# Dilated attention of a hybrid encoder layer: strided scores by residue, softmax halves joined afterwards, projections interleaved

## The chip, the cores and the metric

The kernel runs on one core of a Trainium2 chip. The metric is the device time of one execution in microseconds; the kernel before has a median of 2906.49 us over three runs (2903.2 to 2910.44). All times in the sections up to the prediction come from these runs, from one profiled execution and from its trace.

Names of engines as the profile has them: PE is the matrix engine (PEld its weight loads), DVE the vector engine, ACT the scalar engine, POOL the GpSimd engine, SP the engine whose queue issues most DMAs.

## What is computed

One layer over 1024 tokens of width 2048, float32. The part that matters here is the attention group: 16 heads of width 64, with q and k partly rotated, and three dilated windows that are softmaxed separately and then mixed by their log-denominators (reference, cut):

```python
DILATION_CFG = ((128, 1), (512, 4), (2048, 16))
...
q = rope_partial(heads(aq, ATT_HEADS), pos) * (ATT_HD ** -0.5)
k = rope_partial(heads(ak, ATT_HEADS), pos)
v = heads(av, ATT_HEADS)
res = [dilated_band_attention(q, k, v, w, d) for (w, d) in DILATION_CFG]
outs = jnp.stack([r[0] for r in res])
lses = jnp.stack([r[1] for r in res])
alpha = jax.nn.softmax(lses, axis=0)
o_att = jnp.einsum('gbsh,gbshe->bshe', alpha, outs).reshape(B, S, ATT_W)
y_att = o_att * jax.nn.silu(ag.astype(f32))
```

In each window query i sees keys i + dilation*m with |m| <= 64, so 1, 4 and 16 are the steps. Mixing by the softmax of the log-denominators equals one softmax over all three windows with shared keys counted more than once. Both kernels use that: the windows of step 4 and 16 are one "strided" part (keys of the query's residue modulo 4, 256 of them, with log 2 added where both windows hold the key), and the window of step 1 is the "local" part (256 keys around a block of 128 queries). One softmax row has 512 entries, 256 of each part.

The rest of the layer: a norm, the input projection, an HGRN2 scan (8 heads), the output projection, norms and a gated embedding.

## The kernel before

The program is written with a planner: each engine's instructions are ordered at build time by their place in the program and by a modelled readiness, so that work that stands later in the program is moved ahead where an engine would be idle. Weight pieces are loaded with raised priority (`PRIO`).

Stages: the norm of x and its transposes (`prenorm`), v and the scan's values for all tokens (`v_group`), 8 scan heads (`hgrn`), 8 pairs of attention heads (`att`, 128 columns of q, k, v and gate each), then `w_out` and the gate products over token halves (`y_phase`, `g_phase`).

A projection of 128 columns is a "group" (`group_parts`, from L92): four weight pieces of 4x128 rows, each split into a high and a low fp32r part and a bf16 copy (`piece`, L75 load on SP, L82 ACT, L83 POOL, L84 DVE), each piece multiplied with both token halves in three forms (L101, L102, L106): 96 matmuls of 128x512. It is a generator: it yields twice per piece, so 8 times, after 12 matmuls on average. At its end a `sink` takes the two PSUM banks away. Four banks (`gb`) belong to groups, so two groups are open at most, and four (`wk`) to all else.

`att` does the following for a pair of heads. The k group ends in `sink_k`: `rope_evac` (L520 ACT, four small DMAs per half that swap rows, L527 POOL, L528 DVE), then a split of k into three bf16 parts (L580, L581, L586) and DMAs that copy each head's rows to the other half of the partitions (L582, L584), so that a contraction over 128 rows does two bf16 products at once. The q group does likewise (`sink_q`, `q_parts`), a quarter of the queries at a time. Then 16 units follow, one for each block i of 128 queries and head h (`score`): the strided part in 12 small matmuls (three split products of 32 queries for each of the four residues r; the four outputs stand at the partitions 32r), L634; the local part in three matmuls of 128 queries, L639; mask and row maximum (L645), exponent with row sum (L650), reciprocal (L652) and scaling (L653). Two units later `flip` transposes the 128x512 probabilities (L658, four transposes) and copies them out (L662, L664), and after each eight units `att_pv` multiplies them with the values (L542 strided, L556 local). The gate group (third projection of the pair) is begun before the units (five yields), and its rest stands at the end of the pair's code; the planner takes its matmuls in between the units.

Of the kernel before, what the change touches and what calls it, by code (L numbers as in the profile page):

```python
# [2 lines left out]

# [41 lines left out]
class Kern:  # L45
# [367 lines left out]
    def att_consts(self, positions):  # L413
# [17 lines left out]
        bf = sp.tile([128, 1], F32, name="abf", bufs=1)  # L431
        V.tensor_copy(bf, b)
        tf = sp.tile([128, 1], F32, name="atf", bufs=1)
        V.tensor_copy(tf, tl)
        MK = big.tile([128, 864], F32, name="amask")
        e = self.h2("ae").bitcast(I32)[:, :480]
        nc.gpsimd.iota(e, pattern=[[1, 480]], base=-224, channel_multiplier=0)
        d = self.h2("ad")[:, :480]
        V.tensor_scalar(d, e, bf, None, op0=ALU.subtract)
        V.tensor_copy(e, d)  # L440
        V.tensor_scalar(e, e, 3, None, op0=ALU.bitwise_and)
        c2 = self.h2("ac2")[:, :480]
# [3 lines left out]
        m = MK[:, :480]  # L446
        V.tensor_tensor(m, d, c2, op=ALU.mult)
        V.tensor_tensor(d, d, c2, op=ALU.max)
        V.tensor_scalar(d, d, -NEG, NEG, op0=ALU.mult, op1=ALU.add)
        V.scalar_tensor_tensor(m, m, math.log(2.0), d, op0=ALU.mult, op1=ALU.add)  # L450
        e2 = self.h2("ae2").bitcast(I32)[:, :384]
        nc.gpsimd.iota(e2, pattern=[[1, 384]], base=-128, channel_multiplier=0)
        m = MK[:, 480:]
# [3 lines left out]
        V.tensor_scalar(m, m, -NEG, NEG, op0=ALU.mult, op1=ALU.add)  # L457
# [57 lines left out]
    def rope_evac(self, is_q, hf, src, fin):  # L515
        nc = self.nc
        sl = slice(512 * hf, 512 * hf + 512)
        raw = self.h2("araw")
        sc = 0.125 if is_q else 1.0
        nc.scalar.activation(raw, src, AF.Copy, scale=sc)  # L520
        pt = self.part[self.npart % 2]
        self.npart += 1
        for o in (0, 64):
            nc.sync.dma_start(pt[o:o + 8, :], raw[o + 8:o + 16, :])
            nc.sync.dma_start(pt[o + 8:o + 16, :], raw[o:o + 8, :])
        pr = self.h2("apr")
        nc.gpsimd.tensor_tensor(pr, pt, self.RS[:, sl], op=ALU.mult)  # L527
        nc.vector.tensor_tensor(raw, raw, self.RC[:, sl], op=ALU.mult)  # L528
        fin(raw, pr)
# [5 lines left out]
    def att_pv(self, hf, PT, vc, vn, vix, wstart, yt):  # L535
        nc = self.nc
        o = self.wk("ao")
        ov = o.rearrange("p (i r b) -> p i r b", i=4, r=4)
        for r in range(4):
            for k in range(2):  # L540
                for h in range(2):
                    nc.tensor.matmul(ov[64 * h:64 * h + 64, :, r, :], vc[:, r, k, 64 * h:64 * h + 64],  # L542
                                     PT[h][:, :, k, 32 * r:32 * r + 32], start=(r == 0 and k == 0), stop=False, skip_group_check=True)
        groups = {}
        for i in range(4):
            for ch in range(2):
                groups.setdefault((wstart(4 * hf + i) + 128 * ch), []).append((i, 2 + ch))
        gl = list(groups.items())
        for n, (t, lst) in enumerate(gl):
            for h in range(2):  # L550
                i, ca = lst[0]
                if len(lst) == 2:
                    mv = sap(PT[h][:, :, :, :], i * 512 + 384, [[384, 2], [1, 128]])
                else:
                    mv = PT[h][:, i, ca]
                nc.tensor.matmul(o[64 * h:64 * h + 64, 128 * i:128 * i + 128 * len(lst)], vn[:, vix[t], 64 * h:64 * h + 64], mv,  # L556
                                 start=False, stop=(n == len(gl) - 1), skip_group_check=True)
        nc.scalar.copy(yt[:, 512 * hf:512 * hf + 512].rearrange("p (i b r) -> p i r b", i=4, r=4), ov)


    def att(self, w_in, hp, vsrc, yout):
        nc = self.nc
        V = nc.vector
        big = self.big
        ident = self.ident
        base = 128 * hp
        KS = [big.tile([128, 2, S], BF16, name=f"ak{i}", tag=t, bufs=n) for i, (t, n) in enumerate((("X", 2), ("X", 2), ("O", 1)))]
        QT = big.tile([128, 2, 2, 2, 256], BF16, name="aqt", tag="hv", bufs=1)
        nat = (slice(0, 64), slice(64, 128))

        def sink_k(hf, p):
            def fin(a, b):
                sl = slice(512 * hf, 512 * hf + 512)
                V.tensor_tensor(a, a, b, op=ALU.add)
                for s in range(3):
                    for h in range(2):
                        n, m = nat[h], nat[1 - h]
                        kd = KS[s][n, h, sl]
                        if s < 2:
                            nc.scalar.copy(kd, a[n])  # L580
                            V.tensor_tensor(a[n], a[n], kd, op=ALU.subtract)  # L581
                            nc.sync.dma_start(KS[s][m, h, sl], kd)  # L582
                            if s == 0:
                                nc.sync.dma_start(KS[2][m, h, sl], kd)  # L584
                        else:
                            V.tensor_copy(kd, a[n])  # L586
            self.rope_evac(False, hf, p, fin)

        qn = {}

        def sink_q(hf, p):
            def fin(a, b):
                qn[hf] = self.h2("aq")
                V.tensor_tensor(qn[hf].rearrange("p (i r b) -> p i b r", i=4, r=4),
                                a.rearrange("p (i b r) -> p i b r", i=4, r=4),
                                b.rearrange("p (i b r) -> p i b r", i=4, r=4), op=ALU.add)
            self.rope_evac(True, hf, p, fin)

        def q_parts(j):
            q = qn[j // 2][:, 256 * (j % 2):256 * (j % 2) + 256]  # L600
            for h in range(2):
                n = nat[h]
                qd = QT[n, j % 2, h]
                nc.scalar.copy(qd, q[n, None, :].to_broadcast([64, 2, 256]))
                V.tensor_tensor(q[n], q[n], qd[:, 0], op=ALU.subtract)
            t = big.tile([128, 2, 256], BF16, name="aq23", tag="hacc", bufs=1)
            nc.scalar.copy(t[:, 0], q)
            V.tensor_tensor(t[:, 1], q, t[:, 0], op=ALU.subtract)
            for h in range(2):
                nc.sync.dma_start(QT[nat[1 - h], j % 2, h], t[nat[h]])  # L610

        starts = [0, 128] + [128 * j - 64 for j in range(1, 8)] + [768, 896]
        vix = {t: i for i, t in enumerate(starts)}
        vn = big.tile([128, 11, 128], F32, name="avn", tag="ht", bufs=1)
        vc = big.tile([128, 4, 2, 128], F32, name="avc", tag="hvt", bufs=1)
        for i0, n in ((0, 2), (2, 7), (9, 2)):
            t0 = starts[i0]
            nc.sync.dma_start(vn[:, i0:i0 + n], vsrc[t0:t0 + 128 * n, :].rearrange("(c p) e -> p c e", p=128))
        for k in range(2):
            nc.sync.dma_start(vc[:, :, k], vsrc[512 * k:512 * k + 512, :].rearrange("(p r) e -> p r e", r=4))  # L620
        self.group(w_in, 1024 + base, sink_k)
        self.flush()
        self.group(w_in, base, sink_q)
        q_parts(0)
        q_parts(1)

        yt = big.tile([128, S], F32, name="ayt", tag="gt", bufs=1)
        def score(i, h, sm, first):
            w0 = wstart(i)
            sc = self.wk("asc")  # L630
            qb = QT[:, (i // 2) % 2, h, :, 128 * (i % 2):128 * (i % 2) + 128]
            for s, sq in ((0, 0), (1, 0), (2, 1)):
                for r in range(4):
                    t = nc.tensor.matmul(sc[32 * r:32 * r + 32, :256], qb[:, sq, 32 * r:32 * r + 32],  # L634
                                     KS[s][:, h, r::4], start=(s == 0), stop=False, skip_group_check=True)
                    if first is not None and s == 0:
                        self.after(t, first)
            for s, sq in ((0, 0), (1, 0), (2, 1)):
                nc.tensor.matmul(sc[:, 256:], qb[:, sq], KS[s][:, h, w0:w0 + 256], start=False, stop=(s == 2), skip_group_check=True)  # L639
            ms = 32 * (7 - i)  # L640
            mw = 480 + (w0 - 128 * i + 128)
            mx = self.sp.tile([128, 1], F32, name="amx")
            mk = sap(self.MK[:, :], ms, [[mw - ms, 2], [1, 256]])
            smh = sm[:, h]
            V.tensor_tensor_reduce(out=smh.rearrange("p (a b) -> p a b", a=2), in0=sc.rearrange("p (a b) -> p a b", a=2),  # L645
                                    in1=mk, scale=1.0, scalar=-3.0e38, op0=ALU.add, op1=ALU.max, accum_out=mx)
            nm = self.sp.tile([128, 1], F32, name="anm")
# [30 lines left out]
        for _ in range(5):  # L678
            mm = next(gpart)
# [348 lines left out]
```

## Time and profile before

| | us |
|---|---|
| median of three runs | 2906.49 |
| the profiled execution's own time | 2911.69 |
| its span, first to last instruction | 2909.9 |
| PE busy in it | 2785.7 (96%) |
| DVE, ACT, POOL busy | 1508.4, 925.5, 1023.8 |
| attention before the first `w_out` matmul, 1268.32 to 2050.83 | 782.51, of which PE busy 770.88 |
| one pair of heads, from the same point of one to that of the next | 101.1 |

A busy share is the time that an engine had an instruction in flight. Matmuls overlap in flight (one of 128x512 shows some 390 ns and the next begins some 227 ns later), so what a matmul costs the PE is read from the starts of neighbours, not from its duration.

### The profile page before, as it was taken

Reading aid. Unit: us, or ns where it says so; the run is one execution under the profiler, and the core shown is the slowest. Engines: PE = TensorE matmul, PEld = TensorE weight load, DVE = VectorE, ACT = ScalarE, POOL = GpSimd, SP = SyncE. Lnnn points to the kernel's source line nnn. Section 1 sums busy time; section 2 is a strip of 40 time slices with the busy share of each in tenths; the row PEclk is TensorE's granted clock in tenths of the full one; section 3 lists DMA queues with packets and bytes.
Section 4 is the critical chain, followed back from the end, with each engine's and each line's share of the span. In section 5 each row is a group of like instructions: output and inputs, shape, how many; then the busy total and the mean of one; then the engine's idle time right before and its main releaser. Section 6 shows DMA issues by size and latency. Waiting matters only on the chain. (4 is left out here: it accounts for less than half of the span.)

```text
span 2909.9 us, 46582 instructions
## 1 busy us (share of the span) xinstructions
PE 2785.7 (96%) x18128; PEld 1885.7 (65%) x18384; DVE 1508.4 (52%) x2833; ACT 925.5 (32%) x1672; POOL 1023.8 (35%) x769
## 2 busy tenths in 40 slices
PE   6999999999999999999999999999999899999997
PEld 4666666676667676676666666666566566665664
DVE  8601116856346346356655555555755645555555
ACT  5311112222122112124434444443533223333323
POOL 2422223413313313322222222222244554666555
PEclk9999999999999999999999999999999999999998
DMA  6412221211111111121221222122344543433453
GB/s 226 121 55 80 77 86 39 66 52 39 57 52 44 52 52 45 51 65 55 78 70 45 73 76 71 47 74 71 113 122 133 159 142 97 131 113 109 146 155 106
DMA packets 251614, 250.54 MB, mean 86 GB/s; under 512 B 21633, under 2 KB 175233, under 8 KB 250241
## 3 DMA queue, kind: packets, MB, share of 16 engines
q1 hardware_dynamic: 242224, 238.62, 27.6%
q10 hardware_dynamic: 9168, 8.93, 0.9%
q8 instruction: 144, 2.36, 0.3%
q14 instruction: 78, 0.63, 0.1%
HBM read 205.54 MB, written 29.36 MB: 81 GB/s over the span
## 5 line engine op out<-in xcount | busy, mean ns | idle before, releaser
L83 POOL TENSOR_TENSOR wl<-raw,wh 128x512 fp32r<-128x512 f32 x568 | 764.7, 1350 | 1599.8 <-ACT wh L82 1507.1
L84 DVE CAST wb<-raw 128x512 bf16<-128x512 f32 x584 | 430.5, 740 | 785.2 <-PE gb L106 281.8
L82 ACT CAST wh<-raw 128x512 fp32r<-128x512 f32 x584 | 358.4, 617 | 1241.7 <-PE gb L101 414.7
L101 PE MATMUL gb<-uh,wh 128*128 128x512 f32 x1792 | 744.3, 415 | 0.0
L102 PE MATMUL gb<-uh,wl 128*128 128x512 f32 x1792 | 708.6, 395 | 0.0
L106 PE MATMUL gb<-ul,wb 128*128 128x512 bf16 x1632 | 405.7, 380 | 9.8 <-issue 1.8
L101 PEld LDWEIGHTS gb<-uh,wh 128*128 128x128 f32 x1792 | 337.1, 188 | 82.9 <-issue 1.2
L102 PEld LDWEIGHTS gb<-uh,wl 128*128 128x128 f32 x1792 | 337.1, 188 | 68.9 <-issue 1.0
L106 PEld LDWEIGHTS <-wb 128*128 128x128 bf16 x1792 | 158.4, 98 | 204.6 <-issue 54.3
L810 PE MATMUL gb<-wh,yh 128*128 128x512 f32 x512 | 231.2, 452 | 2.8 <-DVE Y L842 2.8
L810 PE MATMUL gb<-wh,th 128*128 128x512 f32 x480 | 215.8, 450 | 0.0
L811 PE MATMUL gb<-wl,yh 128*128 128x512 f32 x512 | 203.7, 398 | 4.7 <-POOL wl L83 4.7
L811 PE MATMUL gb<-wl,th 128*128 128x512 f32 x480 | 190.6, 397 | 5.4 <-POOL wl L83 5.4
L645 DVE CUSTOM_DVE_ANT_1 asm<-asc,amask 128x512 f32<-128x512 f32 x128 | 88.3, 690 | 119.9 <-PE asc L639 119.7
L814 PE MATMUL gb<-wb,yl 128*128 128x512 bf16 x479 | 133.7, 383 | 1.6
L814 PE MATMUL gb<-wb,tl 128*128 128x512 bf16 x452 | 126.2, 384 | 1.0
L650 ACT ACTIVATE asm<-asm,anm 128x512 f32<-128x512 f32 x128 | 92.5, 722 | 90.3 <-DVE anm L648 90.0
L810 PEld LDWEIGHTS gb<-wh,yh 128*128 128x128 f32 x512 | 97.6, 191 | 33.3 <-DVE Y L842 3.3
L737 PE MATMUL gb<-wh,uh 128*128 128x512 f32 x256 | 116.4, 461 | 1.4 <-ACT wh L82 1.3
L811 PEld LDWEIGHTS gb<-wl,yh 128*128 128x128 f32 x512 | 97.4, 190 | 24.3 <-POOL wl L83 5.9
L738 PE MATMUL gb<-wl,uh 128*128 128x512 f32 x256 | 102.4, 407 | 10.9 <-POOL wl L83 7.9
L634 PE MATMUL asc<-ak,aqt 128*32 128x256 bf16 x1536 | 109.7, 401 | 3.2 <-issue 2.4
(274 smaller groups left out, 3668.4 us busy)
## 6 DMA issues: line engine op xcount, KB each, us to landing
raw<-in_w_in_dram SPq DMA_DIRECT2D x320, 256.0 KB
raw<-in_w_out_dram SPq DMA_DIRECT2D x128, 256.0 KB
raw<-in_w_pg_dram SPq DMA_DIRECT2D x128, 256.0 KB
xt<-in_x_dram SPq DMA_DIRECT2D x8, 1024.0 KB
vD<-vo SPq DMA_DIRECT2D x32, 256.0 KB
raw<-yD SPq DMA_DIRECT2D x32, 256.0 KB
xr<-in_x_dram SPq DMA_DIRECT2D x32, 256.0 KB
ak<-ak SPq DMA_DIRECT2D x96, 64.0 KB
```

Source lines behind the costliest of these rows:

```text
L82: nc.scalar.copy(wh, raw)
L83: (sub or nc.gpsimd).tensor_tensor(wl, raw, f32(wh), op=ALU.subtract)
L84: nc.vector.tensor_copy(wb, raw)
L101: nc.tensor.matmul(pb[hf], wh[:, k], self.uh[hf][:, kt], start=(kt == 0), stop=False)
L102: nc.tensor.matmul(pb[hf], wl[:, k], self.uh[hf][:, kt], start=False, stop=False)
L106: mm = nc.tensor.matmul(pb[hf], wb[:, k], self.ul[hf][:, kt], start=False, stop=(kt == KT - 1))
L634: t = nc.tensor.matmul(sc[32 * r:32 * r + 32, :256], qb[:, sq, 32 * r:32 * r + 32], KS[s][:, h, r::4], start=(s == 0), stop=False, skip_gr ...
L737: nc.tensor.matmul(pb[t], hi, wh, start=(k == 0), stop=False)
L738: nc.tensor.matmul(pb[t], hi, wl, start=False, stop=False)
L810: nc.tensor.matmul(pb[t], a, pc[0], start=first, stop=False)
L811: nc.tensor.matmul(pb[t], a, pc[1], start=False, stop=False)
L814: nc.tensor.matmul(pb[t], lo[:, k, 128 * t:128 * t + 128], pc[2], start=False, stop=last)
```

## The change

Only the attention group is changed.

The strided scores are computed for 128 queries of one residue at a time: a half of the tokens (512) holds 128 queries of each residue, so one full product of 128 queries and 256 keys takes the place of four products of 32 queries. The queries are therefore laid out by residue (`(r i b)` in place of `(i r b)`), and the local products take a copy (`ql`) of them in the old order, made by ACT or POOL. A unit is now (part, i) and holds both heads: six matmuls into one bank.

The rows of the strided and of the local part of a query now stand in different units and on different partitions. Each unit takes its own row maximum and sum over 256 entries; afterwards maxima and sums are copied across between the two layouts (16 small copies), and factors are worked out that join the two (minimum, differences, one exponent, sums, reciprocal). The signs of the scores and masks are turned round, so that the extreme is a minimum and serves as the exponent's bias directly. The scaling by the factors stands in `values`, half of it on ACT and half on DVE, ahead of the transposes.

`att` is replaced by a class `Pair` and an order written out at the bottom: the scores of a half take four yields of a group between their units; the next pair's q group and k group stand inside the pair's own code, the k group ahead of the second `values`; the gate group is spread over the pair.

```diff
-        MK = big.tile([128, 864], F32, name="amask")
+        MK = big.tile([128, 768], F32, name="amask")
...
-        sc = 0.125 if is_q else 1.0
+        sc = -0.125 if is_q else 1.0
...
+        def q_half(self, hf):
...
+            for c in range(2):
+                cs = slice(256 * c, 256 * c + 256)
+                for h in range(2):
+                    n = nat[h]
+                    qd = QT[n, h, :, cs]
+                    nc.scalar.copy(qd, q[n, None, cs].to_broadcast([64, 2, 256]))
+                    V.tensor_tensor(q[n, cs], q[n, cs], QT[n, h, 0, cs], op=ALU.subtract)
...
+        def scores(self, hf, fill):
+            K, KS, QT = self.K, self.KS, self.QT
...
+            for u, (loc, i) in enumerate(((0, 0), (0, 1), (1, 0), (0, 2), (1, 1), (0, 3), (1, 2), (1, 3))):
+                w0 = K.wstart(4 * hf + i)
+                sc = K.wk("asc")
+                if loc:
+                    ql = K.big.tile([128, 4, 4, 32], BF16, name="aql", tag="aql", bufs=3)
+                    src = QT.rearrange("p h s (r i b) -> p (h s) r i b", i=4, r=4)[:, :, :, i]
+                    (nc.gpsimd.tensor_copy if i % 2 else nc.scalar.copy)(ql, src)
+                for h in range(2):
+                    for s, sq in ((0, 0), (1, 0), (2, 1)):
+                        if loc:
+                            st = ql[:, 2 * h + sq].rearrange("p r b -> p (r b)")
+                            mv = KS[s][:, h, w0:w0 + 256]
+                        else:
+                            st = QT[:, h, sq, 128 * i:128 * i + 128]
+                            mv = KS[s][:, h, i::4]
+                        nc.tensor.matmul(sc[:, 256 * h:256 * h + 256], st, mv, start=(h == 0 and s == 0),
+                                         stop=(s == 2), skip_group_check=True)
...
+                for h in range(2):
+                    d = sm[h][:, loc, i]
+                    V.tensor_tensor_reduce(out=d, in0=sc[:, 256 * h:256 * h + 256], in1=K.MK[:, ms:ms + 256], scale=1.0,
+                                           scalar=3.0e38, op0=ALU.add, op1=ALU.min, accum_out=own[:, 0, loc, h, i:i + 1])
+                    nc.scalar.activation(d, d, AF.Exp, scale=-1.0, bias=own[:, 0, loc, h, i:i + 1],
+                                         accum_out=own[:, 1, loc, h, i:i + 1])
+                if u % 2:
+                    next(fill, None)
+            for x in range(4):
+                for y in range(4):
+                    o = oth[32 * x:32 * x + 32].rearrange("p s l h i -> p (s l h) i")[:, :, y]
+                    w = own[32 * y:32 * y + 32].rearrange("p s l h i -> p (s l h) i")[:, :, x]
+                    V.tensor_copy(o, w)
...
+            nc.scalar.activation(e, e, AF.Exp)
...
+        def values(self, hf):
...
+            def turn(n):
+                l, i = steps[n]
+                p = K.wk("apt", (128, 2, 2, 128))
+                for h in range(2):
+                    d = sm[h][:, l, i]
+                    if h:
+                        nc.scalar.activation(d, d, AF.Copy, scale=f[:, l, h, i:i + 1])
+                    else:
+                        V.tensor_scalar(d, d, f[:, l, h, i:i + 1], None, op0=ALU.mult)
+                    for c in range(2):
+                        nc.tensor.transpose(p[:, h, c], d[:, 128 * c:128 * c + 128], K.ident)
+                if n % 2 == 0:
+                    pt[n // 2] = K.big.tile([128, 2, 2, 2, 128], F32, name="aPT", tag=("KD", "hq")[n // 2 % 2], bufs=1)
+                (nc.scalar.copy if n % 2 else V.tensor_copy)(pt[n // 2][:, n % 2], p)
...
+            for n in range(10):
+                if n < 8:
+                    turn(n)
+                if n >= 2:
+                    use(n - 2)
...
-        for hp in range(8):
-            K.att(w_in, hp, vD[hp // 4][:, 128 * (hp % 4):128 * (hp % 4) + 128], yD[hp])
+        heads = [K.Pair(K, w_in, hp, vD[hp // 4][:, 128 * (hp % 4):128 * (hp % 4) + 128], yD[hp]) for hp in range(8)]
+
+        def run(parts, n=8):
+            for _ in range(n):
+                next(parts, None)
+
+        run(heads[0].queries(), 9)
+        K.flush()
+        run(heads[0].keys(), 9)
+        heads[0].q_half(0)
+        for n, a in enumerate(heads):
+            b = heads[n + 1] if n < 7 else None
+            a.loads()
+            g = a.gate()
+            if n == 0:
+                run(g, 4)
+            a.scores(0, g)
+            bq = b.queries() if b else iter(())
+            run(bq, 4)
+            if n == 7:
+                run(g, 2)
+            a.q_half(1)
+            a.values(0)
+            a.scores(1, bq if b else islice(g, 2))
+            run(bq)
+            if b:
+                if n:
+                    run(g, 2)
+                run(b.keys(), 9)
+                b.q_half(0)
+            a.values(1)
+            run(g)
```

`use(n)` multiplies step n's transposed probabilities with the values, four matmuls of 64 columns each (two key blocks, two heads), strided steps with `vc` and local ones with `vn`, all into one bank. `keys`, `queries`, `gate` and `loads` issue what `sink_k`, `sink_q`, `sink_g` and the value loads issued before.

More of the change, by code (lines that the diff above doesn't have):

```diff
@@ L2 @@
 from contextlib import ExitStack, nullcontext
+from itertools import islice
 import numpy as np
@@ L430, in att_consts @@
         V.tensor_tensor(tl, tl, rho, op=ALU.add)
-        bf = sp.tile([128, 1], F32, name="abf", bufs=1)
-        V.tensor_copy(bf, b)
+        pf = sp.tile([128, 1], F32, name="apf", bufs=1)
+        V.tensor_copy(pf, p_i)
         tf = sp.tile([128, 1], F32, name="atf", bufs=1)
         V.tensor_copy(tf, tl)
-        MK = big.tile([128, 864], F32, name="amask")
[L436 to L439, printed above, removed]
+        MK = big.tile([128, 768], F32, name="amask")
+        e = self.h2("ae").bitcast(I32)[:, :384]
+        nc.gpsimd.iota(e, pattern=[[1, 384]], base=-128, channel_multiplier=0)
+        d = self.h2("ad")[:, :384]
+        V.tensor_scalar(d, e, pf, None, op0=ALU.subtract)
         V.tensor_copy(e, d)
         V.tensor_scalar(e, e, 3, None, op0=ALU.bitwise_and)
-        c2 = self.h2("ac2")[:, :480]
+        c2 = self.h2("ac2")[:, :384]
         V.tensor_scalar(c2, e, 0, None, op0=ALU.is_equal)
@@ L445, in att_consts @@
         V.tensor_scalar(d, d, 64.0 * 64.0, None, op0=ALU.is_le)
-        m = MK[:, :480]
+        m = MK[:, :384]
         V.tensor_tensor(m, d, c2, op=ALU.mult)
         V.tensor_tensor(d, d, c2, op=ALU.max)
-        V.tensor_scalar(d, d, -NEG, NEG, op0=ALU.mult, op1=ALU.add)
-        V.scalar_tensor_tensor(m, m, math.log(2.0), d, op0=ALU.mult, op1=ALU.add)
+        V.tensor_scalar(d, d, NEG, -NEG, op0=ALU.mult, op1=ALU.add)
+        V.scalar_tensor_tensor(m, m, -math.log(2.0), d, op0=ALU.mult, op1=ALU.add)
         e2 = self.h2("ae2").bitcast(I32)[:, :384]
         nc.gpsimd.iota(e2, pattern=[[1, 384]], base=-128, channel_multiplier=0)
-        m = MK[:, 480:]
+        m = MK[:, 384:]
         V.tensor_scalar(m, e2, tf, None, op0=ALU.subtract)
@@ L456, in att_consts @@
         V.tensor_scalar(m, m, 64.0 * 64.0, None, op0=ALU.is_le)
-        V.tensor_scalar(m, m, -NEG, NEG, op0=ALU.mult, op1=ALU.add)
+        V.tensor_scalar(m, m, NEG, -NEG, op0=ALU.mult, op1=ALU.add)
         self.MK = MK
@@ L533, in after @@
                                reason="issue order")
[L535 to L539, printed above, removed]
-            for k in range(2):
-                for h in range(2):
[L542 to L558, printed above, removed]
@@ L561, in att @@
[L561 to L572, printed above, removed]
-                sl = slice(512 * hf, 512 * hf + 512)
[L574 to L647, printed above, removed]
-            V.tensor_scalar(nm, mx, -1.0, None, op0=ALU.mult)
-            den = self.sp.tile([128, 1], F32, name="aden")
-            nc.scalar.activation(smh, smh, AF.Exp, bias=nm, accum_out=den)
-            rd = self.sp.tile([128, 1], F32, name="ard")
-            V.reciprocal(rd, den)
-            return V.tensor_scalar(smh, smh, rd, None, op0=ALU.mult)
-        def flip(i, h, sm, PT, mark):
-            p = self.wk("apt", (128, 4, 128))
-            for c in range(4):
-                t = nc.tensor.transpose(p[:, c], sm[:, h, 128 * c:128 * c + 128], ident)
-                if c == 0 and mark is not None:
-                    self.after(t, mark)
-            if h == 0:
-                nc.scalar.copy(PT[h][:, i % 4], p)
-            else:
-                V.tensor_copy(PT[h][:, i % 4], p)
-        def wstart(i):
-            return 0 if i == 0 else (768 if i == 7 else 128 * i - 64)
-        def sink_g(hf, p):
-            sl = slice(512 * hf, 512 * hf + 512)
-            sg = self.h2("sg")
-            nc.scalar.activation(sg, p, AF.Sigmoid)
-            V.tensor_tensor(sg, p, sg, op=ALU.mult)
-            nc.gpsimd.tensor_tensor(sg, sg, yt[:, sl], op=ALU.mult)
-            nc.sync.dma_start(yout[:, sl], sg)
-        gpart = self.group_parts(w_in, 3072 + base, sink_g)
-        for _ in range(5):
-            mm = next(gpart)
-        PTs = {}
-        sms = {}
-        marks = []
-        dist = 2
-        units = [(i, h) for i in range(8) for h in range(2)]
-        for u in range(16 + dist):
-            if u < 16:
-                i, h = units[u]
-                if h == 0:
-                    if i in (2, 4):
-                        q_parts(i // 2 + 1)
-                    sms[i] = big.tile([128, 2, 512], F32, name="asm", tag=("KD", "hq")[i % 2], bufs=1)
-                marks.append(score(i, h, sms[i], mm if u == 0 else None))
-            if u >= dist:
-                pi, ph = units[u - dist]
-                if pi % 4 == 0 and ph == 0:
-                    PTs[pi // 4] = [big.tile([128, 4, 4, 128], F32, name=f"aPT{g}", tag=("F2", "Q2")[g], bufs=1) for g in range(2)]
-                flip(pi, ph, sms[pi], PTs[pi // 4], marks[min(u, 15)])
-                if pi % 4 == 3 and ph == 1:
-                    self.att_pv(pi // 4, PTs[pi // 4], vc, vn, vix, wstart, yt)
-        for _ in gpart:
-            pass
```

117 lines of the change are left out of this document (added).

## The prediction

> **What bounds the kernel now.** I read the page's engine table first, then the stretches of the attention stage, then the PE's waits in it.
>
> ```profile
> span 2909.9 us, 46582 instructions
> PE 2785.7 (96%) x18128; PEld 1885.7 (65%) x18384; DVE 1508.4 (52%) x2833; ACT 925.5 (32%) x1672; POOL 1023.8 (35%) x769
> ```
>
> ```profile
> 1500.34:1601.46 101.12, 99.78 (x698) 65.79 (x705) 56.14 (x135) 45.58 (x85) 24.58 (x19) 1.00 0.23 65
> ...
> 1904.62:2005.70 101.08, 99.74 (x698) 65.78 (x705) 55.81 (x135) 45.70 (x85) 24.58 (x19) 1.00 0.23 65
> ```
>
> ```profile
> PE apt L658 <- DVE asm L653: 3.7, 6, 0.6
> ```
>
> The two rows of stretches are one pair of heads each (columns: length, then busy time of PE, PEld, DVE, ACT, POOL, the granted clock, DMA share, GB/s). Of 101.1 us the PE is busy for 99.75, at full clock; DVE has 56, ACT 46, POOL 25, and the DMAs 0.23. The largest wait that the PE's own list names in the whole stage sums to 3.7 us. So here the time is the PE's instruction stream, and an edit is worth what it takes out of that stream, less what it makes the PE wait.
>
> **The stream of a pair, priced by starts.** Durations overlap, so I price by the starts in the timeline.
>
> ```profile
> 1279.20 0.58 PE L101 MATMUL gb<-uh,wh 128*128 128x512 f32 x1
> ...
> 1284.60 0.58 PE L101 MATMUL gb<-uh,wh 128*128 128x512 f32 x1
> ```
>
> ```profile
> 1342.86 0.60 PE L658 MATMUL apt<-ident,asm 128*128 128x128 f32 x4
> 1343.39 0.87 PE L634 MATMUL asc<-ak,aqt 128*32 128x256 bf16 x12
> 1344.19 0.50 PE L639 MATMUL asc<-ak,aqt 128*128 128x256 bf16 x3
> 1344.45 0.48 PE L101 MATMUL gb<-uh,wh 128*128 128x512 f32 x1
> 1344.76 0.39 PE L102 MATMUL gb<-uh,wl 128*128 128x512 f32 x1
> 1344.99 0.40 PE L101 MATMUL gb<-uh,wh 128*128 128x512 f32 x1
> ```
>
> ```profile
> 1369.67 1.85 PE L542 MATMUL ao<-aPT,avc 128*64 128x128 f32 x29
> ...
> 1373.30 0.39 PE L639 MATMUL asc<-ak,aqt 128*128 128x256 bf16 x2
> ```
>
> ```profile
> L634 PE MATMUL asc<-ak,aqt 128*32 128x256 bf16 x192 | 13.7, 400 | 0.1
> L658 PE MATMUL apt<-ident,asm 128*128 128x128 f32 x67 | 9.9, 273 | 0.6 <-DVE asm L653 0.6
> L639 PE MATMUL asc<-ak,aqt 128*128 128x256 bf16 x48 | 8.2, 276 | 0.0
> L542 PE MATMUL ao<-aPT,avc 128*64 128x128 f32 x64 | 4.8, 277 | 0.0
> L556 PE MATMUL ao<-aPT,avn 128*64 128x128 f32 x32 | 3.2, 273 | 0.0
> L556 PE MATMUL ao<-aPT,avn 128*64 128x256 f32 x16 | 2.5, 379 | 0.0
> ```
>
> - Groups: one weight piece (24 matmuls) takes 1284.60 - 1279.20 = 5.40 us, so one yield 2.70 us, one group 21.6, three groups 64.8.
> - Strided scores: 1344.19 - 1343.39 = 0.80 us for 12 instructions; 16 units make 12.8.
> - Local scores: 0.26 us for three, and the way back to the group costs 0.31 - 0.23 = 0.08 more: 0.34, so 0.114 for one full product; 16 units make 5.4.
> - Transposes: 1343.39 - 1342.86 = 0.53 for four. Their starts lie (0.60 - 0.27)/3 = 0.11 apart, so 0.09 of it is the change to another shape. 16 sets make 8.5.
> - Values: 3.6 us for all but two instructions of a half, some 3.8 with them: 7.6.
>
> The sum is 99.1, plus 1.3 not busy, against 101.1; the rest is other changes of shape.
>
> **The change, part by part.**
>
> *Strided products.* Of 192 instructions of 32 queries and 48 local ones 96 full products are left. At 0.114 each they cost 10.9 where 18.2 stood: -7.3 us a pair, -58 over eight. What the trace doesn't show is a full product whose keys are read with a step of four. The bounds come from these two rows:
>
> ```profile
> L634 PE MATMUL asc<-ak,aqt x1536: 384/405/418, 1330.4 to 2109.2; 128*32 128x256 bf16 x192
> L639 PE MATMUL asc<-ak,aqt x384: 272/273/421, 1331.2 to 2109.7; 128*128 128x256 bf16 x192
> ```
>
> A small product with stepped keys is in flight 405 - 273 = 132 ns longer than a full one with contiguous keys of the same length. If that is the price of four outputs fed at once from four places, it goes. If it is the price of the step, it stays on 384 products: +51 us, which leaves 7. In between I take the first, for the reason in these rows of the scan (four small products at once too, float32):
>
> ```profile
> L275 PE MATMUL pl<-Q,X x64: 210/213/221, 470.5 to 471.2; 128*32 128x32 f32 x64
> L275 PE MATMUL pl<-Q,X x64: 192/196/217, 473.8 to 474.4; 128*32 128x32 f32 x64
> ```
>
> The first reads a moving operand that jumps by some 4 KB at each element, the second one that jumps after every two, and only the first is longer. A far jump for each two elements costs nothing there, and the keys' step is 8 bytes. It is an argument, not a measurement.
>
> The Trainium skill has a rule on either side. "SBUF — State Buffer" (Specifications) says that memory lines of 16 bytes give full bandwidth from two hits on; the scan's two rows agree, and by it the step is free and the sum stays at -58. "TensorE: Matmul & The Clock Gate" (Measured speedup vs the span model) says that tiles side by side take the time of one and about 4 ns for each further one; by it the four outputs were free already, the 132 ns are the step's, and the sum would be -7. The trace's 0.80 us for three sets of four disagree with that span, but not on whose fault it is.
>
> *Values.* Transposes and value products keep their volume: 64 transposes; 128 instructions of 128 columns, where 64 + 32 + 16 double ones stood. But now each of 16 steps changes from transposes to products and back, one change of 0.09 more per step: +1.5 a pair, +12. Against it the 0.114 counts a way back to the group for each three products, 32 a pair, where the written order has 8 (after each second unit): 24 x 0.08 = -1.9 a pair, -15. I let these two cancel.
>
> *Softmax beside the PE.* Rows of one pair:
>
> ```profile
> L650 ACT ACTIVATE asm<-asm,anm 128x512 f32<-128x512 f32 x16 | 11.6, 723 | 12.2 <-DVE anm L648 12.1
> L650 ACT ACTIVATION_READ_ACCUMULATOR asm<-asm,anm 128x1 f32 x16 | 3.0, 186 | 0.0
> L82 ACT CAST wh<-raw 128x512 fp32r<-128x512 f32 x12 | 7.4, 614 | 13.5 <-PE gb L101 11.9 <-POOL apr L527 1.6
> L607 ACT CAST aq<-aq 128x256 bf16<-128x256 f32 x4 | 1.6, 401 | 4.6 <-DMA aqt<-aq 4.1 <-DVE aq L605 0.6
> L645 DVE CUSTOM_DVE_ANT_1 asm<-asc,amask 128x512 f32<-128x512 f32 x16 | 11.1, 692 | 16.8 <-PE asc L639 16.8
> L648 DVE TENSOR_SCALAR anm<-amx 128x1 f32<-128x1 f32 x16 | 2.4, 148 | 0.3
> ```
>
> An exponent of 256 columns lies between 0.36 (half) and 0.72; from 0.614 and 0.401 for 512 and 256 I take 0.723 - 0.213 = 0.51. ACT then has 32 x (0.51 + 0.19) = 22.3 for 14.6, plus 16 scalings at 0.40 and four query copies at 0.61: 45.6 + 7.7 + 6.4 + 2.4 = 62 of some 94 us. DVE has 32 maxima at 0.49 (the same proportion) for 16 at 0.69, loses 16 of the 0.148 operations, 16 reciprocals and half the scaling, and gains some 50 tiny operations at 0.15: it stays under 60. POOL's two copies a half are hidden behind the first yield between the units. None is a bound, and in one half's scores ACT's 16 x 0.70 + 1.2 = 12.4 us stand beside 5.5 of products and 10.8 of four yields.
>
> *Joining.* Sixteen copies across, for which the trace has no row (between 0 and 0.148 each, the nearest row, which I take), nine small operations and an exponent: some 4.2 us after the last unit. Ahead of the first `values` stand four yields (10.8), ahead of the second two yields and the k group (27): hidden, and 4.2 x 16 = 67 us if no cover stood there.
>
> *Groups moved.* The k group issues four weight loads, eight row-swapping DMAs and twelve key copies on SP; it goes from ahead of the pair's own units to the end of the pair before. `loads` waits for the last value products on the same queue, and the next pair's weight pieces stand behind it. What is late next is the key's way from its group to the first score:
>
> ```profile
> L520 ACT ACTIVATE araw<-gb x2: 575/576/577, 1383.1 to 1387.1; 128x512 f32<-128x512 f32 x2
> L582 SPq DMA_DIRECT2D ak<-ak x8: 461/540/548, 1394.4 to 1413.1; - x8
> ```
>
> ```profile
> L520 ACT ACTIVATE araw<-gb x2: 589/593/597, 1415.2 to 1420.1; 128x512 f32<-128x512 f32 x2
> ...
> 1431.46 0.85 PE L634 MATMUL asc<-ak,aqt 128*32 128x256 bf16 x12
> ```
>
> Keys took 30 us (1383.1 to 1413.1), with nobody waiting; the first half of the queries, for which the PE did wait, 16.3 (1415.2 to 1431.46). Both halves of the keys are needed at once, and the halves begin 4.9 apart: I estimate 21. The cover is `values` of the second half, 8 x 0.53 + 3.8 = 8.0, and two gate yields, 5.4: 13.4; with the next pair's first four gate yields, which depend on nothing in it, 24.2. The planner has moved such matmuls forward before: the k group that is evacuated from 1383.1 on is the second pair's, and the first pair's value products of its first half stand at 1369.67, so half of that pair's units were still to come. So I charge 1 us a pair: +8.
>
> **Sum.** -58 + 12 - 15 is taken as -58; + 8 gives -50. The profiled execution took 2911.69 (span 2909.9): 2861.7. The median of the runs lies 5.2 below that execution: 2856.
>
> **Rivals.**
>
> 1. *Step at a loss:* the 132 ns belong to the step. For it: the small products' longer flight is the only trace of stepped bf16 keys. Against: the scan's rows. With 132 ns it gives 2856 + 51 = 2907; with the shortest flight of the row, 384 - 273 = 111 ns, 2899; and without the waits that I charged 2891: I take 2899, between no change and barely faster. The Trainium skill's "TensorE: Matmul & The Clock Gate" stands on this rival's side, "SBUF — State Buffer" against it.
> 2. *Keys late, the slower side:* the key's way, 25 us (between 21 and 30), finds only the 13.4 of its own pair's cover, because weight pieces queue behind `loads`: 11.6 at seven pair boundaries, +81, less the 8 charged: 2929. It decides from (58/7 =) 8.3 us of lateness a pair. For it: SP issues in order. Against: only 1.3 us of a pair is idle now under the same planner.
> 3. *More than forecast:* no new wait, the cancelled terms fall to the good side, and the 1.3 idle goes: 2856 - 8 - 3 - 10 = 2835.
>
> **Chances.** Forecast 0.60, first rival 0.18, second 0.14, third 0.08. What can be told from no change is 0.3%, 8.7 us: under 2897.8 is faster, over 2915.2 slower. Faster: 0.60 + 0.08, and half of the first rival with its bounds, 0.08: 0.76. Same: the rest of that rival and the mild end of the second, 0.11. Slower: 0.13. The range 2828 to 2906 leaves out the second rival and the ends of the others.
>
> **What would show it.** Right: stretches of a pair of 94 to 95 us with the PE still over 98% busy; strided products of 273 ns in flight, starts 0.11 apart. Rival 1: the strided form near 400 ns, the local one at 273. Rival 2: PE idle before the first strided product of each pair, released by a key copy's DMA or by DVE. The joining would be wrong if the first transposes of `values` wait for DVE's or ACT's scaling by several us.

## The result and the profile after

The changed kernel takes 2933.41 us (median of four runs, 2930.28 to 2936.55), the kernel before 2908.47 beside it: a ratio of 1.0088 with a 95% interval of 1.0068 to 1.0108. It is slower by some 25 us. The forecast was 2856 and faster. Medians here and below are over runs at a granted clock of 0.98 to 0.99; one execution of the experiment with a fixed table, at 0.558 and 4581.4 us, is left out.

The page of the changed kernel (engine table), and two pairs of heads from its view of stretches (length, then busy time of PE, PEld, DVE, ACT and POOL, clock, DMA share, GB/s):

```profile
span 2929.7 us, 45661 instructions
PE 2793.9 (95%) x17360; PEld 1906.6 (65%) x17360; DVE 1541.4 (53%) x3265; ACT 1022.2 (35%) x2094; POOL 1045.4 (36%) x801
```

```profile
1733.76:1836.92 103.16, 98.77 (x578) 68.17 (x577) 62.72 (x190) 57.33 (x138) 27.89 (x23) 1.00 0.25 67
...
1940.00:2043.14 103.14, 99.42 (x578) 68.60 (x577) 62.38 (x189) 56.98 (x137) 27.67 (x23) 0.98 0.24 64
```

A pair takes 103.1 us where it took 101.1, with some 120 PE instructions fewer. The PE is no longer busy all the time in it: in the two shown 4.4 and 3.7 us are idle where it was 1.3. DVE and ACT are at 62 and 57, about as reckoned; neither is full.

The two forms of score product in the changed kernel (the three numbers with strokes are the least, the median and the greatest flight in ns):

```profile
L642 PE MATMUL asc<-ak,aqt x384: 385/407/437, 1337.1 to 2088.8; 128*128 128x256 bf16 x192
L642 PE MATMUL asc<-ak,aql x384: 270/273/421, 1337.5 to 2090.3; 128*128 128x256 bf16 x192
```

Same line of the program, same shape, the queries on the left of equal size: the strided form (`aqt`) flies 407 ns, the local one (`aql`) 273. In the timeline they stand like this:

```profile
1743.76 1.53 PE L642 MATMUL asc<-ak,aqt 128*128 128x256 bf16 x6
...
1748.52 1.47 PE L642 MATMUL asc<-ak,aql 128*128 128x256 bf16 x12
```

Six strided products are (1.53 - 0.41)/5 = some 0.225 us apart, twelve local ones (1.47 - 0.27)/11 = 0.109.

What the PE waited for from the end of the scan to the last values, with total, times and longest in us:

```profile
PE asc L642 <- DMA ak<-ak: 16.4, 6, 3.9
PE ao L707 <- ACT aPT L697: 6.8, 5, 1.6
PE asc L642 <- ACT sg L727: 4.5, 2, 2.4
PE apt L694 <- DVE asm L692: 4.2, 3, 2.1
```

Before, the same stretch named 4.2 for the scaling (L653) and 3.1 for a copy of transposes, and 2.4 at the very first score.

To put both effects into one account I took each PE instruction's time from its start to the next one's start, from the last scan output to the first gate product, and counted what goes over 0.48 us as waiting (less 0.24 for the instruction itself):

| us | before | after | difference |
|---|---|---|---|
| whole stretch | 1201.5 | 1223.3 | +21.8 |
| score products | 145.4 | 125.0 | -20.4 |
| transposes | 66.0 | 70.1 | +4.1 |
| value products | 65.6 | 70.9 | +5.3 |
| waiting | 26.4 | 58.6 | +32.2 |
| groups and the rest | 898.1 | 898.7 | +0.6 |

So the scores gave a third of what was reckoned, and waits took more than that back. The experiments go after each.

### The profile page after: what moved, and what is told of

The parts are those of the page before. It is cut to its first block, busy times and chain, and to the rows that moved or that the text cites. A ratio compares the mean times of both kernels' runs of the same rounds, so it can differ in the third digit from the quotient of the medians.

```text
span 2929.7 us, 45661 instructions
## 1 busy us (share of the span) xinstructions
PE 2793.9 (95%) x17360; PEld 1906.6 (65%) x17360; DVE 1541.4 (53%) x3265; ACT 1022.2 (35%) x2094; POOL 1045.4 (36%) x801
## 5 line engine op out<-in xcount | busy, mean ns | idle before, releaser
L85 DVE CAST wb<-raw 128x512 bf16<-128x512 f32 x584 | 406.3, 699 | 769.6 <-PE gb L107 276.5
L107 PE MATMUL gb<-ul,wb 128*128 128x512 bf16 x1792 | 434.8, 381 | 0.2 <-issue 0.2
L647 DVE CUSTOM_DVE_ANT_0 asm<-asc,amask 128x256 f32<-128x256 f32 x256 | 95.8, 422 | 125.0 <-PE asc L642 124.1
L649 ACT ACTIVATE asm<-asm,aown 128x256 f32<-128x256 f32 x256 | 127.3, 498 | 58.1 <-DVE aown L647 57.9
L642 PE MATMUL asc<-ak,aqt 128*128 128x256 bf16 x384 | 96.8, 405 | 20.9 <-DMA ak<-ak 16.4
```

The source lines that it names most:

```text
L85: nc.vector.tensor_copy(wb, raw)
L107: mm = nc.tensor.matmul(pb[hf], wb[:, k], self.ul[hf][:, kt], start=False, stop=(kt == KT - 1))
L649: nc.scalar.activation(d, d, AF.Exp, scale=-1.0, bias=own[:, 0, loc, h, i:i + 1], accum_out=own[:, 1, loc, h, i:i + 1])
```

## Experiments

### The step of the keys

First the same kernel with neighbouring keys in the strided products:

```diff
-                            mv = KS[s][:, h, i::4]
+                            mv = KS[s][:, h, 256 * i:256 * i + 256]
```

> The changed kernel, but each strided product reads 256 neighbouring keys (256*i on) in place of every fourth one; the scores are then of other keys than the reference's, the amount of work is the same. Theory A (the step of the keys doubles a product's time): in flight 273 ns in place of 405, starts 0.11 us apart in place of 0.21, so 384 x 0.10 = 38 us less: 2895, a little faster than the kernel before. Theory B (what lengthens these products is the operand laid out by residue, or the order of the units, not the step): still 405 ns, 2933. If the waits grow by what the products lose (theory C, the softmax behind them is the bound), 273 ns but over 2920.

2898.28 us, a ratio of 0.9973 (0.9961 to 0.9984) to the kernel before, 35 less than the changed kernel. The products' rows:

```profile
L642 PE MATMUL asc<-ak,aqt x384: 269/273/283, 1324.4 to 2058.1; 128*128 128x256 bf16 x192
L642 PE MATMUL asc<-ak,aql x384: 271/273/421, 1331.2 to 2059.4; 128*128 128x256 bf16 x192
```

407 has become 273, and by the account the scores take 86.2 us, 59.2 less than before the change. That is the 58 that was reckoned at a price of 0.114. The step of four alone holds 125.0 - 86.2 = 38.8 us. Theory B is out. Some of C is in it as well: the waits are 68.2 here, 10 more than with the step.

Then the kernel before with the same edit in its small products:

```diff
-                                     KS[s][:, h, r::4], start=(s == 0), ...
+                                     KS[s][:, h, 256 * r:256 * r + 256], start=(s == 0), ...
```

> The kernel before, but its small strided products read 256 neighbouring keys (256*r on) in place of every fourth one; the scores are of other keys than the reference's, the amount of work is the same. Theory A (the step alone): twelve small products then take about the time of three full ones, 0.35 to 0.45 us in place of 0.80, so 128 x 0.35 to 0.45 = 45 to 58 us less: 2850 to 2863. Theory D (four outputs fed at once from four places share the reads, whatever the step): still 0.80, 2908. In between, both count.

2865.19 us, a ratio of 0.9863 (0.9846 to 0.9879). Its rows, and a unit in its timeline:

```profile
L634 PE MATMUL asc<-ak,aqt x1536: 269/273/285, 1329.6 to 2066.6; 128*32 128x256 bf16 x192
```

```profile
1340.26 0.51 PE L634 MATMUL asc<-ak,aqt 128*32 128x256 bf16 x12
1340.71 0.50 PE L639 MATMUL asc<-ak,aqt 128*128 128x256 bf16 x3
```

That is 43 us less, just short of theory A's 45 to 58, and theory D is out. The twelve small products take 0.45 us where they took 0.80: three times 0.109 and some 0.1 for the change of shape behind them. In the trace of this unit the four products of a set start 2 to 5 ns apart, and the next set 0.11 to 0.12 us after the one before. Four outputs side by side cost what one costs; only the step was dear. The rule of the Trainium skill's "TensorE: Matmul & The Clock Gate" (Measured speedup vs the span model) on this, some 4 ns for each further tile, holds here once the step is gone. So the change replaced a form that was not at fault.

How the price runs with the step, in one kernel with a line for each unit:

```diff
...
+                        elif i == 0:
+                            nc.tensor.matmul(dst, st, KS[s][:, h, 0:256], **kw)
+                        elif i == 1:
+                            nc.tensor.matmul(dst, st, KS[s][:, h, 0:512:2], **kw)
+                        elif i == 2:
+                            nc.tensor.matmul(dst, st, KS[s][:, h, 0:768:3], **kw)
+                        else:
+                            nc.tensor.matmul(dst, st, mv, **kw)
```

> The changed kernel with the step of the keys as 1, 2, 3 and 4 for the four strided units i = 0 to 3 of each half, each on a line of its own (scores of other keys than the reference's for the first three). One look at the four groups' flight and starts. Theory A1 (time by the bytes that the step spans): step 1 and 2 at 0.11 us, step 3 at 0.16, step 4 at 0.21. Theory A2 (any step is slow): 2, 3 and 4 all at 0.21. Theory A3 (the time is by step from the second element on): 0.11, 0.11 x 2 capped at 0.21. Theory B: all four alike.

```profile
L647 PE MATMUL asc<-ak,aqt x96: 269/273/283, 1324.9 to 2058.8; 128*128 128x256 bf16 x96
L649 PE MATMUL asc<-ak,aqt x96: 273/275/277, 1325.1 to 2059.5; 128*128 128x256 bf16 x96
L651 PE MATMUL asc<-ak,aqt x96: 328/335/373, 1337.5 to 2065.4; 128*128 128x256 bf16 x96
L653 PE MATMUL asc<-ak,aqt x96: 387/407/421, 1338.9 to 2068.2; 128*128 128x256 bf16 x96
```

Steps of 2 and 4 bytes (L647, L649) are free but for 2 ns, 6 bytes (L651) cost 62 ns more in flight, 8 bytes (L653) 134. The starts of neighbours on one line lie 0.109, 0.114, 0.173 and 0.227 us apart (medians in the trace). That is theory A1: up to 4 bytes a column the step is free, and beyond it the time grows with the bytes that the step spans. Steps of more than 8 bytes were not tried. The rule of the Trainium skill's "SBUF — State Buffer" (Specifications), two hits in a line of 16 bytes for full bandwidth, does not hold for this operand: a step of 8 bytes has two hits and is slow.

### Where the waits come from

With the step gone the changed kernel is still 33 us behind the kernel before with the same edit (2898.28 against 2865.19), and by the account its waits are 68.2 us against 28.4 there. That part is the new order, the split softmax or the steps of `values`.

The longest named wait is for the keys. In the trace of the changed kernel, a pair's start:

```profile
L521 ACT ACTIVATE araw<-gb x2: 598/600/603, 1713.7 to 1719.9; 128x512 f32<-128x512 f32 x2
```

```profile
1733.76 0.58 PE L102 MATMUL gb<-uh,wh 128*128 128x512 f32 x1
1737.42 0.61 PE L642 MATMUL asc<-ak,aqt 128*128 128x256 bf16 x2 [3.08 <-DMA ak<-ak]
```

From the first half's evacuation out of PSUM to the first product are 23.7 us (22.6 to 23.7 over the seven boundaries between pairs), and the PE runs out of other work 3.1 before. A part of this way stands in SP's queue:

```profile
1721.88 0.62 SPq L525 DMA_DIRECT2D apart<-araw  x1
1726.80 1.19 SPq L568 DMA_DIRECT2D ak<-ak  x2
1728.03 0.68 SPq L526 DMA_DIRECT2D apart<-araw  x1
```

```profile
1730.27 1.70 POOL L528 TENSOR_TENSOR apr<-apart,asin 128x512 f32<-128x512 f32 x1 [1.09 <-DMA apart<-araw]
```

The last of the second half's four row-swapping DMAs is issued 6.2 us after the third, behind the first half's six key copies (5.3 to 6.2 at the seven boundaries). The rotation on POOL, with which the second half's keys go on, waits for it. In the kernel before, the four at 1387.71 to 1389.76 were issued one after the other, some 0.7 us apart. No run moved this DMA, so that an earlier one would end the wait is not shown.

The first try put the k group ahead of two gate yields:

```diff
+                run(b.keys(), 9)
                 if n:
                     run(g, 2)
-                run(b.keys(), 9)
```

> The changed kernel with the next pair's k group ahead of the two gate yields instead of behind them, so that the keys have 5.4 us more of other PE work before the next pair's first score. Theory L (the keys come late at the pair's end, some 3 us of PE idle at each of seven boundaries): the idle before the first strided product goes, 15 to 25 us less: 2908 to 2918. Rival (the planner had moved these yields anyway, or the queue of ACT and DVE is what is late): within 5 us of 2933.

2941.87 us (1.0129, 1.0112 to 1.0145): 8 us slower, neither 15 to 25 faster nor within 5 us as the rival had it. Its waits:

```profile
PE asc L642 <- DMA ak<-ak: 20.2, 8, 4.0
PE gb L102 <- ACT araw L521: 10.0, 7, 2.1
PE ao L710 <- DVE aPT L697: 9.0, 8, 1.3
```

The keys are as late as before, and now a group waits for ACT to free its bank and the values wait for DVE. Two yields more in the program were no help: in this trace two of the second half's four row swaps stand behind the first half's key copies (at 1730.45 and 1731.18, with the first swap at 1722.60), and the way from evacuation to first product is 24.6 us at that boundary. Whether the wait itself is worth its time was tried by taking away what it waits for: the scores read a fixed table of the same size and step.

```diff
...
-            K, KS, QT = self.K, self.KS, self.QT
+            K, QT = self.K, self.QT
+            KS = [K.KX] * 3
```

> The changed kernel, but the score products read a fixed table (the rotation's cosines, lower bits cleared, read as bf16, with the same step and sizes) in place of the pair's keys, so no score waits for keys; the keys are still made. The scores are not the reference's. Theory L (the keys come late at the pair's start): the PE's 21 us of named waits ahead of the first strided products go and nothing takes their place: 2910 to 2915. Rival (DVE and ACT are behind at that point anyway, the next wait is as long): 2925 or more.

2917.93 us (1.0038, 1.0023 to 1.0053): some 15 less than the changed kernel, between the two theories. Another wait has grown in its place (the lines of this kernel stand three further down, so L710 is the L707 of the changed one):

```profile
PE ao L710 <- ACT aPT L700: 12.6, 7, 2.1
```

That is the second wait of the list, the first local step of `values`. Around one in the changed kernel ACT and PE read:

```profile
1761.59 0.60 ACT L83 CAST wh<-raw 128x512 fp32r<-128x512 f32 x1
1763.79 1.14 ACT L633 COPY aql<-aqt 128x512 bf16<-128x512 bf16 x2 [1.60 <-DMA aqt<-aq]
1764.83 1.06 ACT L697 COPY aPT<-apt 128x512 f32<-128x512 f32 x2
```

```profile
1763.49 0.66 PE L694 MATMUL apt<-ident,asm 128*128 128x128 f32 x4
1765.46 0.66 PE L707 MATMUL ao<-aPT,avn 128*64 128x128 f32 x8 [1.31 <-ACT aPT L697]
```

ACT does nothing for 1.6 us because the query copies of the second half (L633) wait for a DMA, and the copy-out of transposes that the PE wants (L697) is behind them in its queue. In the program the first `values` stands ahead of these copies; it is the planner that put the copies first. These copies exist only since the change. With all of them on POOL:

```diff
-                    (nc.gpsimd.tensor_copy if i % 2 else nc.scalar.copy)(ql, src)
+                    nc.gpsimd.tensor_copy(ql, src)
```

> The changed kernel with all copies of the queries for the local products on POOL; before, ACT made every second one. Theory Q (ACT takes its instructions in order, and the copies for the second half's scores stand there waiting for the queries' DMA, with the copy-out of the first half's transposes behind them): the PE's wait for ACT's copy-out in the values (6.8 us named in the profile, 1.3 to 1.6 each pair) goes, 7 to 12 us less: 2921 to 2926. Rival: POOL makes them too late and the local scores wait, or the planner shifts the wait elsewhere: 2930 or more.

2931.10 us (1.0082, 1.0061 to 1.0103): no difference from the changed kernel that can be told, as the rival had it. The wait on ACT is gone from the list, but the wait for the keys rose to 20.4 from 16.4. It looks as if each of the two hides part of the other, so both were taken away together:

> The changed kernel with both waits taken away that were taken away singly: scores read a fixed table in place of the pair's keys (with the same step; not the reference's scores), and all query copies are on POOL. Theory (two independent in-order waits, each of which lets the other show): stalls fall from 59 us to about the 26 of the kernel before, 2933 - 30 = 2900 to 2908. Rival (a third wait behind them, the split softmax's own chain of maximum, exponent, exchange and scaling): 2915 or more.

2896.34 us (0.9963, 0.9950 to 0.9976), 37 less than the changed kernel, more than the single edits together and a little more than the theory had. The PE's waits (lines again three further down):

```profile
PE ao L713 <- DVE aPT L700: 3.7, 4, 1.4
PE gb L102 <- ACT araw L523: 2.7, 2, 2.1
PE apt L697 <- DVE asm L695: 2.7, 2, 2.3
```

By the account 28.4 us of waiting are left, against 26.4 in the kernel before. (With the query copies alone moved it was 53.8; with the fixed table alone 39.6, while transposes and value products took 11 us more, in gaps too short for the account to count as waiting.) So the added 32 us of waiting are these two together: keys that are made later than the PE wants them, and copies that block ACT's queue. A third wait of the split softmax is not behind them in this order.

The written order was tried as a cause too, by giving the new arithmetic the old order:

```diff
-        run(heads[0].queries(), 9)
-        K.flush()
-        run(heads[0].keys(), 9)
-        heads[0].q_half(0)
         for n, a in enumerate(heads):
-            b = heads[n + 1] if n < 7 else None
             a.loads()
+            run(a.keys(), 9)
+            if n == 0:
+                K.flush()
+            run(a.queries(), 9)
+            a.q_half(0)
             g = a.gate()
...
+            run(g, 5)
+            a.scores(0, iter(()))
             a.q_half(1)
             a.values(0)
-            a.scores(1, bq if b else islice(g, 2))
...
+            a.scores(1, iter(()))
             a.values(1)
             run(g)
```

> The changed kernel's arithmetic (full products, split softmax) in the order of the kernel before: each pair's own k group, q group, five gate yields, then scores and values of both halves, then the rest of the gate; no next pair's group in a pair's code. Theory O (the written order makes the waits): stalls fall from 59 us to the 26 of the kernel before, so 2933 - 25 to 32: 2901 to 2908. Theory S (the split softmax and the values' steps make them, whatever the order): 2925 or more.

2951.30 us (1.0157, 1.0134 to 1.0180): 18 slower than in the written order, with 71.2 us of waiting.

```profile
PE asc L642 <- issue: 23.2, 8, 3.2
PE apt L694 <- DVE asm L692: 15.4, 15, 2.8
```

The first row is a wait of some 2.9 us ahead of each pair's first score, for nothing that the profile names. That the new unit needs all queries of a half before its first product, where the old one began with a quarter of the tokens, would explain it, but was not tried. Neither of the two waits of the written order is in this list (no key copy, no copy-out by ACT), and larger ones stand in their place. So theory O falls: the old order does not bring the old total of waiting back. The second row is what theory S names, transposes that wait for the scaling by the factors; the written order keeps it at 4.2 us. Which waits appear hangs on the order, then, and the written order is the better of the two for the new units.

### A kernel with the step gone for good

The edit of neighbouring keys only shows a price. The same can be had with the right scores if keys are stored by residue. I built that on the kernel before, with its small products and its order: ACT takes q and k out of PSUM by residue, and tables, key rows, local mask and local values follow.

```diff
-        nc.scalar.activation(raw, src, AF.Copy, scale=sc)
+        nc.scalar.activation(raw.rearrange("p (r j) -> p r j", r=4), src.rearrange("p (j r) -> p r j", r=4), AF.Copy, scale=sc)
...
-                        kd = KS[s][n, h, sl]
+                        kd = KR[s][n, h, :, hf]
...
-                                     KS[s][:, h, r::4], start=(s == 0), ...
+                                     KS[s][:, h, 256 * r:256 * r + 256], start=(s == 0), ...
...
-                nc.tensor.matmul(sc[:, 256:], qb[:, sq], KS[s][:, h, w0:w0 + 256], ...
+                nc.tensor.matmul(sc[:, 256:], qb[:, sq], sap(KS[s][:, h], w0 // 4, [[32, 2], [256, 4], [1, 32]]), ...
```

> The kernel before with its own small products and its own order, complete in what it computes, but with keys stored by residue: ACT takes q and k out of PSUM in that order, the rotation tables, the local mask and the local values follow it, so the strided products read 256 neighbouring keys and the local ones runs of 32. Theory A (the step was the price): as in the run of the kernel before with neighbouring keys, 43 us less, and up to 5 back for nine more value loads a pair and shorter DMA rows: 2865 to 2870. Rival (runs of 32, the strided read of PSUM or the loads cost as much as the step did): 2890 or more.

2886.99 us (0.9929, 0.9912 to 0.9946): faster than both kernels, but with half of the 43 us. The scores take 96.9 us by the account, all that was hoped for; the waits are 45.7, where the kernel before with neighbouring keys had 28.4. Most of the added ones stand at the pairs' first score (13.8 us, released by nothing that the profile names). The value loads are now fourteen a pair in place of five, and they stand ahead of the queries' DMAs in the program. Moved behind the first query parts:

> The kernel before with keys by residue (as in the run of that name, complete), with the pair's 14 value loads moved in the program from ahead of the k group to behind the first query parts. That run lost some 19 of its 43 us to waits, 1.5 to 2 us of them at each pair's first score, whose queries' DMA came late on SP. Theory P (the twelve value loads stand ahead of the row-swapping and query DMAs in SP's queue): the wait goes, 10 to 15 us less than 2887: 2872 to 2877. Rival (the units are now shorter, the PE is simply earlier at the first score than the queries' way of 14 us takes): 2883 or more.

2876.86 us (0.9892, 0.9876 to 0.9909): 10 less, the time that theory P gave. The wait itself is only smaller: of the 9.7 us of waiting that went by the account, 3.8 stood at the first score, where 10.0 are left. Then one gate yield more ahead of the first unit (`range(6)` for `range(5)`):

> The run before this one (keys by residue, values loaded later) with six gate yields ahead of the first unit in place of five, so 2.7 us (or 0.9, the sixth being a short one) more of other PE work for the queries' way. If the PE is early (rival above): the rest of the wait at the first score goes, 8 to 15 us less than the run before this one. If SP was the cause: within 4 us of it.

2872.60 us (0.9882, 0.9867 to 0.9897): 4 less, which the runs of the two hardly tell apart. The wait at the first score is down to 5.4 us, at two places in place of seven; so the PE was early there, as the rival said, but the gain is not the 8 to 15 that it gave. The last kernel's rows:

```profile
L641 PE MATMUL asc<-ak,aqt x1536: 269/273/421, 1334.6 to 2076.3; 128*32 128x256 bf16 x192
```

```profile
PE asc L641 <- issue: 5.4, 2, 4.3
PE ao L546 <- DVE aPT L671: 4.5, 1, 4.5
PE apt L665 <- DVE asm L660: 3.3, 7, 1.0
```

It is 33 us faster than the kernel before beside it (2905.88) and some 61 faster than the changed one. Its waiting is 32.6 us, 6 above the kernel before.

## Why the prediction was wrong, step by step

The forecast was -50 in the attention stage; the account gives +22, a difference of 72.

- *Strided products, 0.114 each.* This step failed: the price in a row of them is 0.225, and 38.8 us of the 72 are this. The bounds were named from the right rows (405 against 273 ns), and the truth lay near the upper one, which had 51 (43 by the shortest flight): starts grew by 0.116, not by the 0.132 of the flights, and not every product stands in a row. I left it for the scan's two rows, whose data are float32 and whose moving operand of 32 columns jumps: they were not the nearest rows. The nearest was the same keys with the same step in the small products, and it said 405. Rival 1 was right in its cause. The 58 us reckoned without the step were right to 1 us: with neighbouring keys it was 59.2.
- *What the small products' length meant.* I thought of either four outputs or the step; it was the step wholly.
- *New waits, 1 us a pair.* This failed too: +32 in place of +8, so 24 of the 72. The keys' way was estimated at 21 us and took 22.6 to 23.7; the mistake was to believe that the planner would fill the gap with the next pair's gate. It did so in part, and 2.5 to 3.7 us from start to start at each boundary stayed. Rival 2 had the place right, with a smaller price than its 81 us. SP's queue is in it, but not by its loads: those of the pair's values are issued at 1728.81 to 1731.77, while the second half's rotation waits or runs, and what stood 6 us late there was a row swap behind key copies. The second wait, ACT's queue behind the query copies, was in no step: I had costed the copies only as ACT's time (2.4 us a pair), and not asked what waits behind them and for what they wait.
- *Transposes and values.* +12 for the changes of shape was about right (9.4), but the -15 set against it did not come (groups +0.6): 10 of the 72. The 0.114 was taken to hold a way back to the group for each three products; full products in a row are 0.109 apart without any, so there was next to nothing to take off.
- *Softmax beside the PE.* DVE at 62 and ACT at 57 of 103 us against "under 60" and 62: near enough, and neither is a bound. The joining's chain was hidden as said: the transposes of `values` waited 4.2 us in all for the scaling, as much as before.
- *Rivals as alternatives.* The two rivals don't exclude one another, and both came true in part: 38.8 + 24 on top of the forecast. The range ended at 2906 because each was laid beside the forecast alone.

## What to carry to other kernels

If a matmul is in flight longer than others of its shape, look first at how its moving operand is read, and try it with neighbouring elements before its shape is rebuilt. A copy added to an engine that has time to spare is not free if it waits for a DMA and something that the matrix engine wants stands behind it. A late operand is traced back queue by queue, the DMA queue's order included. Rivals with different causes can come true together, and the range has to hold their sum.

## What the runs showed of the hardware

- A bf16 matmul of 256 columns is in flight for 273, 275, 335 and 407 ns with its moving operand at steps of 2, 4, 6 and 8 bytes; in a row of them the starts are 0.109, 0.114, 0.173 and 0.227 us apart.
- Four bf16 products with 32 outputs each, side by side with four different moving operands, take about as long as one with 128 if each reads neighbouring elements: 273 ns in flight, starts 2 to 5 ns apart, and the next four some 0.11 us later.
- Local keys read as runs of 32 neighbouring bf16 with jumps between them are as fast as one run of 256: the local products of the last kernel with keys by residue show a median of 273 ns too, as in the row below.

```profile
L646 PE MATMUL asc<-ak,aqt x384: 272/273/421, 1335.0 to 2076.7; 128*128 128x256 bf16 x192
```
